# A row maximum that skips NaN: other piece sizes, fewer stores, and loads issued in turn from two queues

## The chip, the cores and the metric

The kernel runs on one core of a Trainium2 chip. Four of the core's engines matter here: ScalarE (ACT in the profile), GpSimd (POOL), VectorE (DVE) and SyncE (SP), which only issues DMA transfers. The data is moved by 16 DMA engines. The metric is the time of one execution on the device, in microseconds (us); the median of ten runs is given.

## The reference

```python
batch, seq, dim = 32, 2048, 2048
x = np.random.randn(batch, seq, dim).astype(np.float32)
mask = np.random.rand(batch, seq, dim) < 0.1
x[mask] = np.nan
...
return np.nanmax(x, axis=-1).astype(np.float32)
```

There are 65,536 rows of 2048 float32 numbers, 537 MB, of which a tenth are NaN. Of each row the largest number that is not NaN is returned (NaN for a row that has no other), so 65,536 results.

## The kernel before

**Groups and tiles.** A group is a block of consecutive rows of x, spread over the 128 partitions. A tile holds up to seven rows per partition, so 7 x 2048 numbers of 4 bytes in each partition, 7 MB in all; the buffers of this tile, `xt`, are three (pool `io`). There are 74 tiles in 13 groups. The table `TILES` says of each tile how it is loaded (rows per transfer), in which pieces it is converted (rows per piece), and in which groups of rows it is reduced. For example `([7], [1, 2, 2, -1, 1], [1, 2, 2, 2])` is one transfer of seven rows, five pieces, four reductions. The first tile has one row; 59 whole tiles of this kind follow, then a taper of 14 tiles with ever smaller transfers and pieces. Tiles are counted from 0 in this document.

**What is done to a piece.** [...] ScalarE reads the upper 16 bits of each number of a piece as an integer and writes a 16-bit key into a second buffer, `kt` (line 116; pool `mid`, four buffers of two rows). The key is an affine function of the upper half that has another slope for NaN patterns, so that turned back they are very low numbers. A second pass turns the key back and writes it over the upper half in `xt`: on GpSimd (line 133), or, for a piece with a minus sign in the table, on ScalarE (line 125). This second pass is called the write-back here. When all pieces under a group of rows are written back, VectorE takes their maximum (line 144) into the group's `acc`.

**End of a group.** VectorE marks rows that held nothing but NaN (line 155) and sets their bits to NaN (line 164) in `fin`; the store of `fin` is queued.

**Order.** Each engine works through its instructions in the order of its program and waits on semaphores for the others; a framework places the instructions and adds the waits. All loads are issued by SP (line 103), each as soon as VectorE has done the last reduction of the tile that had the same buffer three tiles earlier. SP also issues the stores (line 109, two groups late, between the loads; the last two at line 169).

Of the kernel before, what the change touches and what calls it, by code (L numbers as in the profile page):

```python
# [1 line left out]

# [4 lines left out]

TILES = (
    [([1], [1], [1])]
    + [([7], [1, 2, 2, -1, 1], [1, 2, 2, 2])] * 59
    + [([7], [2, 2, 1, 2], [4, 1, 2])]
    + [([7], [1, 2, 2, -2], [3, 2, 2])]
    + [([7], [1, 2, 2, 2], [3, 2, 2])]
    + [([7], [2, 2, 2, -1], [2, 2, 2, 1])]
    + [([2, 5], [1, 1, 2, 2, 1], [1, 1, 2, 2, 1])]
    + [([4, 3], [2, -2, 1, 1, 1], [2, 3, 2])]  # L20
    + [([4, 3], [2, 2, 2, -1], [2, 2, 3])] * 3
    + [([1, 3, 3], [1, 1, 1, 1, 2, -1], [1, 2, 1, 3])]
    + [([3, 2, 2], [1, 1, 1, 1, 1, 1, 1], [2, 1, 1, 1, 1, 1])]
    + [([2, 1, 2, 1, 1], [1, 1, -1, 1, 1, 1, 1], [3, 2, 1, 1])]
    + [([1, 1, 1, 1, 1, 1, 1], [1, 1, -1, 1, 1, 1, 1], [3, 1, 1, 1, 1])]
    + [([1, 1, 1, 1, 1, 1, 1], [1, 1, -1, 1, 1, 1, -1], [1, 2, 1, 1, 1, 1])]
)

GROUPS = [TILES[:7]] + [TILES[i : i + 6] for i in range(7, 73, 6)] + [TILES[73:]]
WIDE = 7  # L30
PIECE = 2

TOP = 0x7F7F
NAN = 0x7FC0
LOW = -129

EDGE = TOP + 0.25

NONE = -255.0 * 2.0**120


@with_exitstack
def kernel(
    ctx: ExitStack,
    tc: tile.TileContext,
    x: bass.AP,
    axis: bass.AP,
    out: bass.AP,  # L50
):

    nc = tc.nc
    P = nc.NUM_PARTITIONS
    f32, i32 = mybir.dt.float32, mybir.dt.int32
    i16, u16 = mybir.dt.int16, mybir.dt.uint16
    ALU = mybir.AluOpType
    ACT = mybir.ActivationFunctionType

    nd = len(x.shape)
    assert axis in (-1, nd - 1), axis
    D = x.shape[-1]  # L70

    xr = x.bitcast(i32).flatten_outer_dims()
    R = xr.shape[0]
    of = out.bitcast(i32).flatten_outer_dims().rearrange("r c -> (r c)")
    rows = [sum(sum(loads) for loads, _, _ in g) for g in GROUPS]
    assert R == P * sum(rows)

    io = ctx.enter_context(tc.tile_pool(name="io", bufs=3))
    mid = ctx.enter_context(tc.tile_pool(name="mid", bufs=4))
    res = ctx.enter_context(tc.tile_pool(name="res", bufs=3))  # L80
    sing = ctx.enter_context(tc.tile_pool(name="sing", bufs=1))
    flag = ctx.enter_context(
        tc.tile_pool(name="flag", bufs=2, space=bass.MemoryType.PSUM)
    )
    top = sing.tile([P, 1], f32)
    nc.vector.memset(top, EDGE)  # L86
    warm = sing.tile([P, 1], f32)
    nc.scalar.activation(out=warm, in_=top, func=ACT.Prelu, alpha=0.5)  # L88

    stores = []  # L90
    r0 = 0
    for s, g in zip(rows, GROUPS):
        xg = xr[r0 : r0 + P * s].rearrange("(p s) d -> p (s d)", p=P)
        og = of[r0 : r0 + P * s].rearrange("(p s) -> p s", p=P)
        r0 += P * s
        acc = res.tile([P, s], f32, tag="acc")
        base = 0
        for loads, pieces, reds in g:
            assert sum(loads) == sum(abs(c) for c in pieces) == sum(reds)
            xt = io.tile([P, WIDE * D], i32, tag="xt")  # L100
            at = 0
            for c in loads:
                nc.sync.dma_start(  # L103
                    out=xt[:, at * D : (at + c) * D],
                    in_=xg[:, (base + at) * D : (base + at + c) * D],
                )
                at += c
            if len(stores) > 1:
                nc.sync.dma_start(**stores.pop(0))
            at = done = 0  # L110
            reds = list(reds)
            for c in pieces:
                back, c = c < 0, abs(c)
                xp = xt[:, at * D : (at + c) * D]
                kt = mid.tile([P, PIECE * D], u16, tag="kt")
                nc.scalar.activation(  # L116
                    out=kt[:, : c * D],
                    in_=xp.bitcast(i16)[:, 1::2],
                    func=ACT.Prelu,
                    bias=top,  # L120
                    scale=-1.0,
                    alpha=float(TOP - LOW) / (EDGE - NAN),
                )
                if back:
                    nc.scalar.activation(  # L125
                        out=xp.bitcast(i16)[:, 1::2],
                        in_=kt[:, : c * D],
                        func=ACT.Copy,
                        bias=float(TOP),
                        scale=-1.0,  # L130
                    )
                else:
                    nc.gpsimd.tensor_scalar(  # L133
                        out=xp.bitcast(i16)[:, 1::2],
                        in0=kt[:, : c * D],
                        scalar1=-1.0,
                        scalar2=float(TOP),
                        op0=ALU.mult,
                        op1=ALU.add,
                    )  # L140
                at += c
                while reds and done + reds[0] <= at:
                    n = reds.pop(0)
                    nc.vector.tensor_reduce(  # L144
                        out=acc[:, base + done : base + done + n],
                        in_=xt[:, done * D : (done + n) * D]
                        .bitcast(f32)
                        .rearrange("p (c d) -> p c d", c=n),
                        axis=mybir.AxisListType.X,
                        op=ALU.max,  # L150
                    )
                    done += n
            base += at
        none = flag.tile([P, s], i32, tag="none")
        nc.vector.tensor_scalar(  # L155
            out=none,
            in0=acc,
            scalar1=NONE,
            scalar2=float(0x00C00000),
            op0=ALU.is_equal,  # L160
            op1=ALU.mult,
        )
        fin = res.tile([P, s], i32, tag="fin")
        nc.vector.tensor_tensor(  # L164
            out=fin, in0=acc.bitcast(i32), in1=none, op=ALU.bitwise_or
        )
        stores.append(dict(out=og, in_=fin))
    for st in stores:
        nc.sync.dma_start(**st)


# [1 line left out]
_INS = ['x', 'axis']  # L173
_OUTS = [((32, 2048), 'float32')]

_NUMBERS = {'axis': -1}


# [26 lines left out]
```

## Time and profile before

| | us |
|---|---|
| median of 10 runs | 1262.38 (1262.19 to 1262.47) |
| the profiled execution, its own time | 1262.31 |
| its span in the profile | 1260.5 |
| VectorE busy | 1127.1 |
| ScalarE busy | 1123.5 |
| GpSimd busy | 1063.0 |
| ScalarE idle before line 116, waiting for a load | 126.0 |

The span runs from the first to the last instruction of the program on the core; the time of an execution has a little around it (here 1.8 us). Busy times of the engines overlap, so they don't add up to the span. The DMA engines moved 537.25 MB, 426 GB/s over the span. In the views, a row of a group ends with the number of instructions, their busy time in us and the mean of one in ns, and the idle time of the engine before them with what ended it.

### The profile page before, as it was taken

Reading aid. Unit: us, or ns where it says so; the run is one execution under the profiler, and the core shown is the slowest. Engines: PE = TensorE matmul, PEld = TensorE weight load, DVE = VectorE, ACT = ScalarE, POOL = GpSimd, SP = SyncE. Lnnn points to the kernel's source line nnn. Section 1 sums busy time; section 2 is a strip of 40 time slices with the busy share of each in tenths; the row PEclk is TensorE's granted clock in tenths of the full one; section 3 lists DMA queues with packets and bytes.
Section 4 is the critical chain, followed back from the end, with each engine's and each line's share of the span. In section 5 each row is a group of like instructions: output and inputs, shape, how many; then the busy total and the mean of one; then the engine's idle time right before and its main releaser. Section 6 shows DMA issues by size and latency. Waiting matters only on the chain.

```text
span 1260.5 us, 1707 instructions
## 1 busy us (share of the span) xinstructions
DVE 1127.1 (89%) x319; ACT 1123.5 (89%) x440; POOL 1063.0 (84%) x302
## 2 busy tenths in 40 slices
DVE  1888998989899998889999898898989879999999
ACT  3898998889899888889889888998888989899997
POOL 2888888888888888888888888888888888998996
DMA  9999999999999999999999999999999999999995
GB/s 412 437 437 437 433 426 422 437 437 437 434 435 435 425 428 437 434 437 435 435 434 426 426 437 435 437 436 433 433 419 437 435 437 435 418 434 430 426 421 211
DMA packets 16141, 537.25 MB, mean 426 GB/s; under 512 B 3456, under 2 KB 3456, under 8 KB 3456
## 3 DMA queue, kind: packets, MB, share of 16 engines
q1 hardware_dynamic: 16128, 537.14, 98.9%
q14 instruction: 13, 0.11, 0.0%
HBM read 536.87 MB, written 0.26 MB: 426 GB/s over the span
## 4 chain that ended last, share of the span: by engine, by line
DMA 51%; POOL 15%; ACT 14%; DVE 10%; issue 9%; SPq 0%; DVEq 0%; ACTq 0%
DMA xt<-in_x_dram 51%; POOL xt L133 15%; ACT kt L116 13%; DVE acc L144 10%; ACT xt L125 1%; SPq L103 0%; DVEq L144 0%; DVE none L155 0%; ACTq L116 0%; DVE fin L164 0%; ACTq L125 0%
## 5 line engine op out<-in xcount | busy, mean ns | idle before, releaser
L144 DVE TENSOR_REDUCE acc<-xt 128x2 f32<-128x4096 f32 (+2 forms) x292 | 1122.8, 3889 | 129.5 <-POOL xt L133 129.3
L133 POOL TENSOR_SCALAR xt<-kt 128x2048 int16<-128x2048 uint16 (+1 forms) x298 | 1062.8, 3567 | 189.3 <-ACT kt L116 175.9
L116 ACT ACTIVATE kt<-xt,top 128x2048 uint16<-128x2048 int16 (+1 forms) x368 | 951.2, 2658 | 128.5 <-DMA xt<-in_x_dram 126.0
L125 ACT ACTIVATE xt<-kt 128x2048 int16<-128x2048 uint16 x70 | 177.7, 2539 | 0.3
L155 DVE TENSOR_SCALAR none<-acc 128x42 int32<-128x42 f32 (+2 forms) x13 | 2.6, 202 | 0.5
L164 DVE TENSOR_TENSOR fin<-acc,none 128x42 int32<-128x42 int32 (+2 forms) x13 | 2.6, 196 | 0.4
L88 ACT ACT_TABLE_LOAD x1 | 1.3, 1283 | 0.7 <-PEq L186 0.7
L86 DVE MEMSET top<- 128x1 f32 x1 | 0.1, 59 | 0.8 <-PEq L186 0.8
L186 POOL MEMSET const-float32-0.0<- 128x1 f32 x1 | 0.1, 98 | 0.2 <-issue 0.2
L88 ACT ACTIVATE warm<-top 128x1 f32<-128x1 f32 x1 | 0.2, 202 | 0.0
L186 POOL MEMSET const-bfloat16-1.0<- 128x1 bf16 x1 | 0.1, 101 | 0.0
L186 POOL MEMSET const-uint8-127<- 128x1 uint8 x1 | 0.1, 101 | 0.0
L186 POOL MEMSET const-float32-1.0<- 128x1 f32 x1 | 0.1, 98 | 0.0
## 6 DMA issues: line engine op xcount, KB each, us to landing
xt<-in_x_dram SPq DMA_DIRECT2D x63, 7168.0 KB, 26.7
xt<-in_x_dram SPq DMA_DIRECT2D x7, 3072.0 KB, 25.6
xt<-in_x_dram SPq DMA_DIRECT2D x19, 1024.0 KB, 20.8
xt<-in_x_dram SPq DMA_DIRECT2D x4, 4096.0 KB, 19.6
xt<-in_x_dram SPq DMA_DIRECT2D x5, 2048.0 KB, 27.6
xt<-in_x_dram SPq DMA_DIRECT2D x1, 5120.0 KB, 23.2
out_dram<-fin SPq DMA_DIRECT2D x11, 21.0 KB, 26.5
out_dram<-fin SPq DMA_DIRECT2D x1, 21.5 KB, 26.8
```

The lines of the kernel that those rows point to most:

```text
L86: nc.vector.memset(top, EDGE)
L88: nc.scalar.activation(out=warm, in_=top, func=ACT.Prelu, alpha=0.5)
L116: nc.scalar.activation(out=kt[:, : c * D], in_=xp.bitcast(i16)[:, 1::2], func=ACT.Prelu, bias=top, scale=-1.0, alpha=float(TOP - LOW) / (E ...
L125: nc.scalar.activation(out=xp.bitcast(i16)[:, 1::2], in_=kt[:, : c * D], func=ACT.Copy, bias=float(TOP), scale=-1.0,)
L133: nc.gpsimd.tensor_scalar(out=xp.bitcast(i16)[:, 1::2], in0=kt[:, : c * D], scalar1=-1.0, scalar2=float(TOP), op0=ALU.mult, op1=ALU.add,)
L144: nc.vector.tensor_reduce(out=acc[:, base + done : base + done + n], in_=xt[:, done * D : (done + n) * D] .bitcast(f32) .rearrange("p (c d ...
L155: nc.vector.tensor_scalar(out=none, in0=acc, scalar1=NONE, scalar2=float(0x00C00000), op0=ALU.is_equal, op1=ALU.mult,)
L164: nc.vector.tensor_tensor(out=fin, in0=acc.bitcast(i32), in1=none, op=ALU.bitwise_or)
L186: nc = _bacc.Bacc("TRN2", target_bir_lowering=False, num_devices=1)
```

## The change

The table of tiles is another one: the 57 whole tiles up to the taper are converted in pieces of two, three and two rows (three instructions on ScalarE in place of five), and the reductions match the pieces. In every third of them ScalarE writes back the last piece, two rows; in the others GpSimd writes back all seven. Before, ScalarE wrote back one row of every such tile. The key buffers hold three rows and are three in number; a piece is put into the buffer in use if it still fits. There are six groups instead of 13, each with an `acc` of its own, on which the marking works in place, and all stores stand after the loop in the program text. Loads are written into the program two tiles ahead of the tile that is worked on, and whole-tile loads are issued in turn by SP and by ScalarE; a tile that is loaded in several transfers stays with the queue whose turn it is and leaves the turn there.

```diff
+    + [
+        ([7], [2, 3, 2], [2, 3, 2]),
+        ([7], [2, 3, 2], [2, 3, 2]),
+        ([7], [2, 3, -2], [2, 3, 2]),
+    ] * 19
+    + [([7], [2, 3, 2], [2, 3, 2])] * 2
+    + [([1, 6], [-1, 3, 1, -2], [4, 3])]
+    + [([7], [3, 2, -2], [3, 4])]
+    + [([7], [2, 2, 3], [2, 2, 3])] * 2
+    + [([7], [2, 1, 2, 2], [2, 1, 2, 2])]
+    + [([5, 2], [1, 1, 1, 2, -1, 1], [1, 1, 1, 3, 1])]
...
-GROUPS = [TILES[:7]] + [TILES[i : i + 6] for i in range(7, 73, 6)] + [TILES[73:]]
+GROUPS = [TILES[:14]] + [TILES[i : i + 12] for i in range(14, 74, 12)]
 WIDE = 7
-PIECE = 2
+
+KEYS = 3
...
-    mid = ctx.enter_context(tc.tile_pool(name="mid", bufs=4))
-    res = ctx.enter_context(tc.tile_pool(name="res", bufs=3))
+    mid = ctx.enter_context(tc.tile_pool(name="mid", bufs=3))
+    res = ctx.enter_context(tc.tile_pool(name="res", bufs=1))
...
+    ready = []
+    queues = [nc.sync, nc.scalar]
+
+    def fetch():
+
+        xg, base, loads = ahead.pop(0)
+        xt = io.tile([P, WIDE * D], i32, tag="xt")
+        queue = queues[0]
+        if len(loads) == 1:
+            queues.reverse()
+        at = 0
+        for c in loads:
+            queue.dma_start(
+                out=xt[:, at * D : (at + c) * D],
+                in_=xg[:, (base + at) * D : (base + at + c) * D],
+            )
+            at += c
+        ready.append(xt)
+
+    stores = []
+    used = KEYS
...
-            xt = io.tile([P, WIDE * D], i32, tag="xt")
-            at = 0
-            for c in loads:
-                nc.sync.dma_start(
-                    out=xt[:, at * D : (at + c) * D],
-                    in_=xg[:, (base + at) * D : (base + at + c) * D],
-                )
-                at += c
-            if len(stores) > 1:
-                nc.sync.dma_start(**stores.pop(0))
+            while len(ready) < 3 and ahead:
+                fetch()
+            xt = ready.pop(0)
...
-                kt = mid.tile([P, PIECE * D], u16, tag="kt")
+                if used + c > KEYS:
+                    kt = mid.tile([P, KEYS * D], u16, tag="kt")
+                    used = 0
+                kp = kt[:, used * D : (used + c) * D]
+                used += c
                 nc.scalar.activation(
-                    out=kt[:, : c * D],
+                    out=kp,
...
-        fin = res.tile([P, s], i32, tag="fin")
-        nc.vector.tensor_tensor(
-            out=fin, in0=acc.bitcast(i32), in1=none, op=ALU.bitwise_or
-        )
-        stores.append(dict(out=og, in_=fin))
+        bits = acc.bitcast(i32)
+        nc.vector.tensor_tensor(out=bits, in0=bits, in1=none, op=ALU.bitwise_or)
+        stores.append(dict(out=og, in_=bits))
     for st in stores:
         nc.sync.dma_start(**st)
```

The rest of the taper's table is changed in the same manner and left out here.

## The prediction

> **What bounds the kernel now.** I read the page first: engine shares, then the slices.
>
> ```profile
> DVE 1127.1 (89%) x319; ACT 1123.5 (89%) x440; POOL 1063.0 (84%) x302
> DMA  9999999999999999999999999999999999999995
> GB/s 412 437 437 437 433 426 422 437 437 437 434 435 435 425 428 437 434 437 435 435 434 426 426 437 435 437 436 433 433 419 437 435 437 435 418 434 430 426 421 211
> q1 hardware_dynamic: 16128, 537.14, 98.9%
> ```
>
> No engine is full, but the DMA engines are busy in every slice but the last, on one queue, at up to 437 GB/s. The transfer sets the time. In the timeline ScalarE starts successive tiles at 481.19, 498.12 and 515.07, so a seven-row load takes T = 16.94 us. Then the chain of waits, one loop of a buffer (start, length, what):
>
> ```profile
> 498.06 0.02 ACTq L116
> ...
> 498.12 5.61 ACT kt L116 x2
> ...
> 503.81 4.76 POOL xt L133
> ...
> 508.65 4.78 POOL xt L133
> ...
> 517.78 4.42 DVE acc L144
> ...
> 522.22 27.32 DMA xt<-in_x_dram
> ...
> 549.62 5.61 ACT kt L116 x2
> ```
>
> A tile that landed at 498.1 is reduced at 522.2, a hold of 24.1, and at once the next load into its buffer is issued. That load lands 27.3 later though it needs 16.94: it stands behind the load in front. This standing time is what keeps the DMA full. Its limit: three buffers make 3T = 50.8; a load that finds the engines idle needs T + 1.9 (the packet records have the first bytes 1.0 after the first issue, and a landing seen 0.85 after a typical engine's last byte). So a hold may last 50.8 - 18.8 = 32.0. Now 8 us are spare. Who holds the loads back is in the waits of the DMA queue (us in total, times, longest):
>
> ```profile
> SPq L103 <- DVE acc L144: 950.5, 59, 24.1
> ```
>
> Prices, from the groups by form (mean ns after the comma):
>
> ```profile
> L144 DVE TENSOR_REDUCE acc<-xt 128x2 f32<-128x4096 f32 x199 | 873.3, 4416 | 95.8 <-POOL xt L133 95.8
> L133 POOL TENSOR_SCALAR xt<-kt 128x4096 int16<-128x4096 uint16 x142 | 676.8, 4766 | 79.5 <-ACT kt L116 73.3
> L116 ACT ACTIVATE kt<-xt,top 128x4096 uint16<-128x4096 int16 x144 | 525.2, 3694 | 8.5 <-DMA xt<-in_x_dram 8.5
> L116 ACT ACTIVATE kt<-xt,top 128x2048 uint16<-128x2048 int16 x224 | 438.3, 1992 | 120.1 <-DMA xt<-in_x_dram 117.6 <-POOL xt L133 2.5
> L133 POOL TENSOR_SCALAR xt<-kt 128x2048 int16<-128x2048 uint16 x156 | 386.1, 2475 | 109.8 <-ACT kt L116 102.6
> L144 DVE TENSOR_REDUCE acc<-xt 128x3 f32<-128x6144 f32 x9 | 58.9, 6548 | 3.3 <-POOL xt L133 3.2
> L125 ACT ACTIVATE xt<-kt 128x4096 int16<-128x4096 uint16 x2 | 9.5, 4770 | 0.1
> ```
>
> Last, how ScalarE's queue treats a wait; the write-back's line, between 519 and 536:
>
> ```profile
> L125 ACTq EVENT_SEMAPHORE  x1: 17/17/17, 519.7 to 519.7; - x1
> L125 ACT ACTIVATE xt<-kt x1: 2470/2470/2470, 528.0 to 528.0; 128x2048 int16<-128x2048 uint16 x1
> ```
>
> The queue was past the write-back's first wait 8.3 us before it ran, so it runs ahead of the datapath; but the ACTq record of 498.06 shows that it stands still at a tile's first activation until that tile has landed. I assume that a load in this queue does likewise: it can overtake activations still executing, not a wait in front of it.
>
> **What the Trainium skill says.** "DMA: Bandwidth & Descriptors", Queues, rings and completion order: SP and ACT own one ring each on the same 16 DMA engines, and an engine with work on both takes packets from them in turn. The run before has one data queue and can't show it. Same page, Where 436 GB/s comes from: a ceiling of 435 GB/s; the best slices have 437, so a second queue finds no spare rate. "Perfetto Trace Analysis", DMA Instruction — HWDGE (DVE, Sync): the issuing sequencer waits for the semaphores itself; the 950.5 us of SP agree.
>
> **The change part by part.**
>
> *Stores*: 12 inside the stream become 5 (the built order puts those five between SP's loads, only the last behind them), plus one at the end in both. A store lengthens a loop of the chain by 0.1 to 0.7 (26.64 without, 27.32 with): 7 x 0.4 = -3 us. A store now has twice the bytes and as many rows; bounds -5 to 0.
>
> *Pieces.* A three-row activation isn't in the trace: at least the two-row 3.69, at most 3 x 1.99 = 5.98; the step from one to two rows is 1.70, so 5.40. On GpSimd the step is 2.29: 7.06 (4.77 to 7.43). A 2,3,2 tile with all its write-back on GpSimd costs it 4.77 + 7.06 + 4.77 = 16.6, as much as T; every third tile costs it 11.8. Over six tiles GpSimd has 90.0 + 1.3 of handovers, VectorE 92.3, ScalarE 86.3, all under 6T = 101.6, so none becomes the bound by sum. But the hold grows: 3.7 (ScalarE, two rows) + 16.6 + 4.4 (VectorE) + 0.3 = 25.0 if GpSimd is free at landing, near 30 where it isn't. These edits cost nothing while the hold stays under 32.0.
>
> *Write-back.* In the built order of ScalarE the write-back of 18 of the 19 tiles that have one stands behind the next tile's first activation, which waits for that tile's landing. Such a tile holds its buffer for T + 3.7 + 4.8 + 4.4 = 29.9 at the least. Every other time (tiles 9, 15, 21...) VectorE also reduces the next tile's first piece before it, and a load stands in ScalarE's queue between.
>
> *Loads on ScalarE.* Tiles 1, 3, 5 ... 59, 62 and 64 are loaded from there. Nine of these (11, 17 ... 59) stand behind the first activation of the tile before: issued when the load in front has already landed, they restart an idle DMA, 1.9 us each. Issue itself (0.33 on SP) is hidden beside activations.
>
> *Two rings.* A load issued while another runs takes half the rate from it. Work is conserved, but the load in front lands later by as much as it had left, and holds everything behind its landing.
>
> I follow engines and queues in the built order, each instruction starting when its engine is free and its last input there. The same count of the order before gives 1261.3 against a span of 1260.5. After the start the new order repeats every six tiles; from tile 16's landing as 0:
>
> - Load 17 (ScalarE) issued at 0, lands 18.8.
> - ScalarE: 16's first piece to 3.7, 15's write-back to 8.4, 16's others to 13.7 and 17.3. VectorE, still busy with 15's middle to 10.5, reduces 16's first to 14.8, 15's last to 19.1: tile 15 held for 38. Load 18 (SP) issued there, 2.1 us of idle DMA after load 17's last byte.
> - GpSimd ends 16 at 25.7, VectorE at 31.8: load 19 issued (ScalarE). Load 18 has 4.2 left, which takes 8.5 shared: lands 42.3.
> - GpSimd runs 17 from 25.7 to 42.5, VectorE ends it at 48.6: load 20 (SP). Load 19 has 4.4 left: lands 59.3.
> - 18's write-back waits for that: 59.3 + 3.7 + 4.7, reduced at 72.2: load 21 (ScalarE), 2.3 idle after load 20, which lands 71.8. Load 21 lands 91.1.
> - 19's second piece waits behind that write-back (to 73.0), GpSimd to 85.0, VectorE to 91.1: load 22 (SP), 1.9 idle; lands 109.9.
>
> So 109.9 in place of 101.6: 8.3 lost per six tiles, eight times from tile 10 to tile 58: +66. The start: loads 1 and 2 share the engines, so tile 1 lands at 36.5 (before, 22.6), is done at 63.6, and the DMA idles 9.7 from 55.0 for want of a buffer; tile 10 is 10.6 late. After tile 58: one more restart (1.9), and 6.3 idle before load 64, which waits for tile 61: +8. The end behind the last landing (12.1 before), with VectorE more behind: +3. Stores -3. Sum 66 + 11 + 8 + 3 - 3 = +85: a span of 1345.5. The profiled execution took 1262.31 with a span of 1260.5, and the median of runs is 1262.38, so I add 1.9: **1347 us**, 6.7% slower.
>
> **Rivals.**
> 1. *Loads keep their order*: the load in front keeps the engines. For: SP alone does so now. Against: the skill's page. The cycle then is 105.6 (restart of load 17 and late load 18 alone), the start costs nothing: +32, 1295.
> 2. *ScalarE's queue waits for the activations in front of a load to end.* For: no run shows a load there. Against: the 8.3 us of running ahead. Each blocked load comes 3.7 later, others too: the count gives +20 more, 1367.
> 3. *Not slower*: two rings together carry more than one. In the same count, break-even is at T = 14.4, 510 GB/s; nothing above 437 is in the slices. If it did, 1255 or so.
> 4. Three-row prices at their bounds: GpSimd at 7.43 and ScalarE at 5.98 give 1358, at 5.5 and 4.5 they give 1334 (1280 with rival 1).
>
> **How the numbers follow.** Shared rings as counted 0.64 (1325 to 1362); rival 1, or something between it and sharing, 0.22 (1278 to 1325); rival 2 0.09; a milder loss, 1265 to 1278, 0.02; rival 3 0.03. The range 1284 to 1368 leaves out about 0.15. A measurement tells about 0.2% (2.5 us) from no change; faster 0.02, same 0.01, slower 0.97.
>
> **What would show it.** Two data queues; slices near 400 GB/s instead of 435, the second one far lower; ScalarE's loads landing 19 to 27 us after issue; ScalarE waiting for landings much longer than 126 us; write-backs of two rows starting right behind a landing; three-row GpSimd at 7.06. Wrong, if a seven-row load in the middle lands at intervals of 16.94 throughout (holds below 32), or if loads of both queues in flight land one T apart (no sharing).

## The result and the profile after

The changed kernel takes 1350.99 us (median; 1347.58 to 1353.88), before 1262.37 on the same chip: a ratio of 1.0705, 95% interval 1.0695 to 1.0714. The prediction was 1347, 6.7% slower. Its profiled execution has a span of 1351.7 us.

The page of the changed kernel, engine shares, slices and data queues:

```profile
DVE 1116.7 (83%) x242; ACT 1053.5 (78%) x281; POOL 1090.0 (81%) x219
DMA  9999999999989989999998999998999999799995
GB/s 411 434 406 434 382 382 431 382 382 407 389 378 414 431 363 386 433 380 384 407 395 366 431 404 387 382 433 367 393 417 399 380 408 434 330 432 434 426 427 235
q1 hardware_dynamic: 10080, 302.26, 52.8%
q10 hardware_dynamic: 4608, 234.88, 41.2%
```

VectorE and ScalarE do less work than before, GpSimd 27 us more (1063.0 before), and none of the three is busy for more than 83% of the span. The rate falls to 363 to 395 GB/s in more than half of the slices between start and taper, and returns to 426 to 434 in the taper, but for one slice with 330. So most of the loss is in the stretch of whole tiles, and it is lost transfer time. The second queue is q10. The shares of the queues say more: the 16 engines were busy for 94.0% of 1351.7 us, before for 98.9% of 1260.5. So they stood still for 81 us in place of 14, and the same bytes took them 1271 us in place of 1247. Of the 91 us of loss in the profile, 67 are idle DMA engines and 24 are packets that took longer.

The waits of the DMA queue of SP, and those of ScalarE, in the changed kernel (us in total, times, longest):

```profile
SPq L117 <- DVE acc L175: 973.6, 36, 37.9
ACT kt L147 <- DMA xt<-in_x_dram: 273.3, 56, 20.6
```

ScalarE waits 273 us for landings in place of 126. The 37.9 can't be set beside the 24.1 of before, as SP now has only every second load: the run below with write-backs in their place and two queues has the same 37.9 and loses nothing in the middle. The holds can be compared. From the landing of a tile to the issue of the next load into its buffer, the median is 31.8 us and the longest 39.5; before, both were 24.2. The prices of the new forms (count, busy us, mean ns):

```profile
L164 POOL TENSOR_SCALAR xt<-kt 128x6144 int16<-128x6144 uint16 x63 | 443.3, 7037 | 115.1 <-ACT kt L147 110.9 <-DVE acc L175 1.8
L147 ACT ACTIVATE kt<-xt,top 128x6144 uint16<-128x6144 int16 x63 | 340.3, 5402 | 19.8 <-POOL xt L164 12.6 <-DMA xt<-in_x_dram 7.2
L156 ACT ACTIVATE xt<-kt 128x4096 int16<-128x4096 uint16 x21 | 99.7, 4750 | 2.2 <-DVE acc L175 2.1
```

7.04, 5.40 and 4.75: those of the prediction were 7.06, 5.40 and 4.77. Its six-tile cycle can be read in the chain of waits. Tile 16 lands at 293.3, tile 22 at 404.4:

```profile
293.36 19.42 DMA xt<-in_x_dram
...
312.86 12.18 ACT kt L147 x3
325.04 27.72 DMA xt<-in_x_dram
...
352.84 3.71 ACT kt L147
356.55 4.65 ACT xt L156
361.20 5.27 ACT kt L147
...
384.52 19.85 DMA xt<-in_x_dram
...
404.48 19.61 DMA xt<-in_x_dram
```

Three of the transfers shown take 19.4 to 19.9 from issue to landing: they were issued when the load in front had landed, or half a microsecond before it. Before, the seven-row loads of tiles 4 to 59 took 26.3 to 27.6, some 10 us of that standing in line. The middle lines are the late write-back: tile 19 lands at 352.8, its first piece runs, then 18's write-back, and only then its own second piece. The landings of the cycle, counted from tile 16's:

| load of tile | 17 | 18 | 19 | 20 | 21 | 22 |
|---|---|---|---|---|---|---|
| predicted | 18.8 | 42.3 | 59.3 | 71.8 | 91.1 | 109.9 |
| measured | 19.5 | 42.6 | 59.5 | 72.6 | 91.8 | 111.1 |

How ScalarE's queue handles a load shows in the timeline (start, us, engine, line):

```profile
293.34 3.71 ACT L147 ACTIVATE kt<-xt,top 128x4096 uint16<-128x4096 int16 x1 [5.17 <-DMA xt<-in_x_dram]
293.36 0.33 ACTq L117 DMA_DIRECT2D xt<-in_x_dram  x1
...
296.95 4.75 ACT L156 ACTIVATE xt<-kt 128x4096 int16<-128x4096 uint16 x1
```

The load of tile 17 is issued 0.02 us after the activation in front of it has begun, not after it has ended, but it could not be issued before tile 16 had landed. VectorE had freed its buffer 3.3 us earlier. Nine loads are held back in this way (11, 17 ... 59), by 2.7 to 3.3 us each. This decides rival 2.

That the two rings share the engines can be read from loads 18 and 19, the only two issued between 309 and 330:

```profile
L117 SPq DMA_DIRECT2D xt<-in_x_dram x1: 328/328/328, 311.2 to 311.2; - x1
L117 ACTq DMA_DIRECT2D xt<-in_x_dram x1: 334/334/334, 325.0 to 325.0; - x1
...
DMA to landing us min/median/max: 24.6/26.1/27.7
```

Load 18 was issued 1.5 us before load 17 landed, and landed 24.6 later, at 335.8. Load 17, which had the engines to itself, took 19.4; five loads of the run below with all write-backs late and no load blocked, issued 1.6 to 2.0 us before the landing in front and undisturbed after it, took 19.3 to 19.8. So load 18 lost some 5 us to the load issued 13.8 after it, which a queue in order would not have allowed. The taking of turns that the Trainium skill describes ("DMA: Bandwidth & Descriptors", Queues, rings and completion order) is there. The packets of the first loads, in the last section, show the turns themselves.

### The profile page after: what moved, and what is told of

It is laid out like the page before. It is cut to its first block, busy times and chain, and to the rows that moved or that the text cites. A ratio compares the mean times of both kernels' runs of the same rounds, so it can differ in the third digit from the quotient of the medians.

```text
span 1351.7 us, 1217 instructions
## 1 busy us (share of the span) xinstructions
DVE 1116.7 (83%) x242; ACT 1053.5 (78%) x281; POOL 1090.0 (81%) x219
## 4 chain that ended last, share of the span: by engine, by line
DMA 53%; ACT 21%; DVE 11%; POOL 9%; issue 5%; SPq 0%; ACTq 0%; DVEq 0%
DMA xt<-in_x_dram 53%; ACT kt L147 17%; DVE acc L175 11%; POOL xt L164 9%; ACT xt L156 4%; SPq L117 0%; ACTq L147 0%; DVE acc L195 0%; DVE none L186 0%; ACTq L117 0%; DVEq L175 0%
## 5 line engine op out<-in xcount | busy, mean ns | idle before, releaser
L164 POOL TENSOR_SCALAR xt<-kt 128x4096 int16<-128x4096 uint16 (+2 forms) x215 | 1089.8, 5069 | 252.1 <-ACT kt L147 238.9
L147 ACT ACTIVATE kt<-xt,top 128x4096 uint16<-128x4096 int16 (+2 forms) x247 | 930.3, 3822 | 286.4 <-DMA xt<-in_x_dram 273.3
L156 ACT ACTIVATE xt<-kt 128x4096 int16<-128x4096 uint16 (+1 forms) x32 | 127.1, 3972 | 2.5 <-DVE acc L175 2.1
## 6 DMA issues: line engine op xcount, KB each, us to landing
xt<-in_x_dram SPq DMA_DIRECT2D x31, 7168.0 KB, 23.2
xt<-in_x_dram SPq DMA_DIRECT2D x13, 1024.0 KB, 22.5
xt<-in_x_dram SPq DMA_DIRECT2D x1, 6144.0 KB, 19.9
```

The source lines that it names most:

```text
L147: nc.scalar.activation(out=kp, in_=xp.bitcast(i16)[:, 1::2], func=ACT.Prelu, bias=top, scale=-1.0, alpha=float(TOP - LOW) / (EDGE - NAN),)
L156: nc.scalar.activation(out=xp.bitcast(i16)[:, 1::2], in_=kp, func=ACT.Copy, bias=float(TOP), scale=-1.0,)
L164: nc.gpsimd.tensor_scalar(out=xp.bitcast(i16)[:, 1::2], in0=kp, scalar1=-1.0, scalar2=float(TOP), op0=ALU.mult, op1=ALU.add,)
```

## The experiments

The theory had three parts that come together in the changed program: late write-backs, ScalarE's loads that wait for a landing ("blocked"), and two rings. The prediction gave most of the loss to the rings: without sharing (its rival 1) it counted 32 of 85 us. The experiments take the parts one by one. In the edits shown, the arguments are shortened: `NO_SYNC` is an order that the framework keeps without adding a semaphore.

**All loads on SP.**

```diff
-    queues = [nc.sync, nc.scalar]
+    queues = [nc.sync, nc.sync]
```

> All loads from SP; pieces, table, groups and buffers as changed. In the order that the framework now builds, each write-back of ScalarE stands right behind its piece, and all six stores stand behind the last load. Theory (two rings together with late write-backs and blocked loads push holds past 32): the hold of every tile is 27.4 by the count, so the DMA never idles in the middle: 1258 us (1255 to 1262), a little under before, landings 16.94 apart. Rival (the pieces of two and three rows alone are too long for three buffers, whatever the queue): 1295 or more, DMA idle in the middle.

1261.36 us, ratio to before 0.9992 (0.9983 to 1.0001): the whole loss is gone, and the gain of 4 us that was counted isn't there; 1 us or nothing. The median hold is 27.3. The pieces, buffers and groups of the change cost nothing by themselves. The framework that places the instructions reacts to the loads on ScalarE: without them it puts each write-back right behind its piece. So this one word undoes two things, and the next runs separate them.

**The old pieces with two queues.** The changed program with the table of before.

> The changed program with its two queues, key buffers and six groups, but the old table of pieces (1, 2, 2, 1, 1, one row written back by ScalarE in each whole tile). Theory: holds are 24.1 as before, so two rings alone cost nothing after the start: 1260 with the start as the changed kernel really has it, 1270 if loads 1 and 2 share from the beginning. Rival (two rings alone cost 4% or more, by lower rate or by restarts): 1310 or more.

1264.39 us, 1.0017 (1.0011 to 1.0024), between the two figures of the theory. Two rings alone cost 2 us. The median hold is 24.1 here and no load is blocked. Loads do share: between tiles 10 and 58 landings follow each other at 12.7 to 21.2 us, but at 17.0 in the mean, as before the change. So neither the new pieces nor the second queue loses much alone.

**Write-backs in their place, two queues.** An order without a semaphore is added on ScalarE:

```diff
+                if last is not None:
+                    tc.add_manual_dep(key.ins, last, NO_SYNC, reason="order")
+                    last = None
                 if back:
-                    nc.scalar.activation(
+                    wb = nc.scalar.activation(
...
+                    last = wb.ins.name
```

> The changed kernel, two queues, with one added order on ScalarE: a write-back stands before the next key activation of the program. The loads then stand behind the last piece of a tile and not behind the next tile's landing, too. Theory: holds 27.4, no idle in the middle: 1261 (1258 to 1273), nearly all of the loss gone. Rival (sharing of the engines by two rings is enough for the loss, whatever the order on ScalarE): 1320 or more.

1269.28 us, 1.0055 (1.0040 to 1.0070), in the stated range. 82 of the 89 us are gone with both queues still in use. Sharing is not enough for the loss. The 7 us left are not in the middle: tile 10 lands at 179.8 here and at 174.9 with one queue, tile 58 at 995.5 and 989.8. Some 5 are lost at the start, the rest behind.

**Late write-backs, one queue.** All loads on SP, and each two-row write-back ordered behind the next tile's first key activation:

```diff
+                if late is not None and late[1] is not xt:
+                    tc.add_manual_dep(late[0], key.ins.name, NO_SYNC, reason="order")
+                    late = None
...
+                    if loads == [7] and pieces == [2, 3, -2]:
+                        late = (wb.ins, xt)
```

> All loads from SP, and every write-back of the 19 tiles of 2, 3 and 2 rows is put behind the first key activation of the next tile, as in the changed kernel. Theory: the hold is 31.7 by the count, just under the limit of 32.0 of the prediction; 1258 if that limit is right; the changed kernel's restarts took about 0.6 longer than counted, which would put the limit at 31.4 and cost up to 0.3 to 0.6 for each of 57 tiles: 1275 to 1295. Rival (a late write-back alone brings the whole loss): 1340 or more.

1302.25 us, 1.0313 (1.0288 to 1.0337), above both ranges of the theory and below the rival. The late write-backs alone cost 41, with one ring. This was the surprise: by the prediction's limit (32.0) they should have been free. A loop of this run, in its chain of waits:

```profile
318.83 21.20 DMA xt<-in_x_dram
...
343.73 4.75 ACT xt L167
348.48 5.27 ACT kt L148
...
353.82 7.05 POOL xt L177
...
360.89 4.89 DVE acc L188
...
367.36 4.42 DVE acc L188
...
371.80 21.71 DMA xt<-in_x_dram
```

The tile lands at 340.0 and is free at 371.8: a hold of 31.8, as counted (the median of the run is 31.7). But the loads take 21.2 and 21.7, not 18.8, although these two are issued 3 us before the load in front has landed (the median of the run is 4.1). 31.8 + 21.7 = 53.5 is three times 17.8, and 17.77 is the mean interval of landings here, 16.94 the full rate.

An idle DMA is the smaller part of this loss. The queue's bytes and share of time, with the write-backs in place (span 1259.4) and late (span 1303.4), one ring in both:

```profile
q1 hardware_dynamic: 14688, 537.14, 98.9%
```

```profile
q1 hardware_dynamic: 14688, 537.14, 97.7%
```

The engines stand still for 30 us in place of 14, and are busy for 1273 us in place of 1246 with the same packets. So 16 of the 44 us between these two executions are idle time, and 28 are packets that took longer.

**Late write-backs of one row, one queue.** As the run before, with another table:

```diff
-        ([7], [2, 3, -2], [2, 3, 2]),
+        ([7], [2, 3, 1, -1], [2, 3, 2]),
```

> As the run with late write-backs on one queue (1302), but ScalarE writes back one row in place of two in every third tile (its last piece is cut into two of one row, GpSimd writes back the other), so the late write-back takes 2.5 in place of 4.75. The hold by the count is 29.4, between the 27.3 of the run on one queue that lost nothing and the 31.7 of the run that lost 0.83 us per load. If a load must be issued 21.5 us before its landing, as that run's loads took, the limit is 50.8 - 21.5 = 29.3, and this run is on it: 1261 to 1268. If the limit is the 32.0 of the prediction and the 41 us came from something else in the late order: 1290 or more, as there. If loads begin to lose gradually from 27.4 on: 1275 to 1285.

1261.06 us, 0.9990 (0.9983 to 0.9997). The write-back is as late as in the run before, but 2.3 us shorter, and 41 us are gone. The median hold is 29.35 (27.3 with write-backs in place, 31.7 with two rows late). The seven-row loads of these runs on one queue, write-backs in place, late with one row, late with two rows (the last number is the median from issue to landing):

```profile
xt<-in_x_dram SPq DMA_DIRECT2D x63, 7168.0 KB, 23.5
```

```profile
xt<-in_x_dram SPq DMA_DIRECT2D x63, 7168.0 KB, 21.6
```

```profile
xt<-in_x_dram SPq DMA_DIRECT2D x63, 7168.0 KB, 21.7
```

From a hold of 27.3 to 29.4, the load gives up 1.9 us of standing in line, and nothing is lost. From there to 31.7 it has nothing left to give: some 21.6 is what a load takes. The limit of the hold lies between 29.4 and 31.7 by these runs, and 50.8 - 21.6 = 29.2 puts it near the lower end. Of the versions run this has the lowest median, 0.1% below before.

**Loads first, two queues.** On ScalarE the load of tile n+1 is ordered before the first key activation of tile n, so that none is blocked.

```diff
+                if at == 0 and ahead_load is not None:
+                    tc.add_manual_dep(key.ins, ahead_load, NO_SYNC, reason="order")
```

> The changed kernel, two queues, with one added order on ScalarE: the load of tile n+1, where it is ScalarE's, stands before the first key activation of tile n, so none waits for a landing. In the order that is built then, two of every three write-backs still stand behind the next tile's first activation, one in its place. Theory (late write-backs and two rings): by the count 1292, and with loads on the edge dearer than counted, as in the run with late write-backs on one queue, 1292 to 1325. Rival (the blocked loads are the cause): 1265 or less. Rival (they are no part of it): 1345 or more.

1311.19 us, 1.0384 (1.0368 to 1.0400), in the range of the theory. 40 us back, but nine of the 19 write-backs (tiles 9, 15 ... 57) went into their place too, more than expected. So the same with all of them late:

> Two queues; all write-backs of the tiles of 2, 3 and 2 rows behind the next tile's first key activation, as changed; but ScalarE's load of tile n+1 stands before the first key activation of tile n, so that no load waits for a landing. Beside the run with late write-backs on one queue (1302) and the changed kernel (1351) it splits their difference. Theory of the prediction (sharing by two rings makes it, the blocked loads are only where it shows): 1335 to 1350. Rival (the blocked loads make it): 1302 plus the 5 to 8 us that two rings cost with early write-backs, 1305 to 1315.

1317.62 us, 1.0447 (1.0426 to 1.0467): 33 us less than the changed kernel, with all write-backs late and both rings in use. The rival is the nearer one: 33 of the 49 us between one queue with late write-backs (1302) and the changed kernel (1351) are the blocked loads; the second ring has 15. Both are differences of a few runs that spread over 6 to 8 us. The queues' shares say what a blocked load does: in this run the engines stand still for 3.3% of 1313.0, 43 us, in the changed kernel for 81, and they are busy for 1270 us in both. So the blocked loads cost idle DMA time. Of the 9.6 us between this profiled execution and that of the late run on one queue, 0.8 are there by tile 10, and 6.3 come behind tile 58, where loads 62 and 64 are still ScalarE's.

**Blocked loads, write-backs in their place, two queues.** The order of the run of 1269, and in addition the loads of tiles 11, 17 ... 59 each behind the first key activation of the tile before. These are the nine that are blocked in the changed kernel.

```diff
+            if n < 9 or n > 59 or n % 6 != 4:
+                behind = None
...
+                if at == 0 and behind is not None:
+                    tc.add_manual_dep(behind, key.ins.name, NO_SYNC, reason="order")
```

> Two queues and write-backs in their place (the run of 1269), but two of three of ScalarE's loads stand behind the first key activation of the tile before and so wait for its landing, with some 15 to 18 such loads over the run. Each restarts an idle DMA: 1.9 to 2.6 us for each, 1269 plus 30 to 45, 1299 to 1314, whatever the rings do. Rival (a blocked load is caught up by the next, which then stands longer in line): 1270 to 1280.

1311.93 us, 1.0393 (1.0377 to 1.0408): +43 for blocked loads with the write-backs in place, at the upper end of what was expected. But they are more, and blocked longer, than in the changed kernel. After VectorE had freed their buffers, the nine chosen loads waited 4.6 to 5.4 us, and eight others (13, 19 ... 55), which this built order puts behind a landing too, 6.8 to 8.2: 103 us in all, of which 43 were lost. In the changed kernel it was 27 us on nine loads. Together:

| write-backs | loads | rings | us |
|---|---|---|---|
| in place | free | one | 1261.4 |
| in place | free | two | 1269.3 |
| late | free | one | 1302.3 |
| in place | blocked, 17 loads | two | 1311.9 |
| late | free | two | 1317.6 |
| late | blocked, 9 loads | two (the change) | 1351.0 |

Late write-backs cost 41 with one ring and 48 with two, blocked loads 33 with late write-backs, two rings 8 to 15. The 43 of blocked loads with write-backs in place is not the same quantity as the 33, so that the sums come near each other proves little. A load can be blocked only in ScalarE's queue: none was blocked with one ring, so the 33 includes whatever sharing a blocked load sets off. All loads on ScalarE would show blocked loads on one ring; that was not run.

**First four loads from SP, two queues, write-backs in place.**

```diff
+        first = len(ahead) > len(TILES) - 5
-        if len(loads) == 1:
+        if len(loads) == 1 and not first:
```

> The changed kernel with the write-backs in their place, as in the earlier run that gave 1269, and the first four loads all from SP, the turns beginning with the fifth. Theory (the rest of that run's loss is at the start, where two rings share while the buffers are first filled): 1262 to 1265. Rival (it is spread over the run): 1269.

1271.41 us, 1.0069 (1.0056 to 1.0083): no gain. Tiles 0 to 3 land as before the change, but tile 4 lands at 77.4 in place of 73.4 and tile 10 at 182.3. From tile 10 to tile 58 landings are 16.97 apart, and nothing more is lost. So the loss isn't spread over the run, nor is it bound to the first four loads; it comes soon after the turns begin. Why was not followed further.

**Six groups alone.** The kernel before, with only the groups, the marking in place and the stores after the loop. Of the edit, the groups:

```diff
-GROUPS = [TILES[:7]] + [TILES[i : i + 6] for i in range(7, 73, 6)] + [TILES[73:]]
+GROUPS = [TILES[:14]] + [TILES[i : i + 12] for i in range(14, 74, 12)]
```

> The kernel before with only the six groups, the marking in place in an acc of its own for each group, and all stores after the loop; the old pieces, four key buffers, loads from SP. In the built order all six stores stand behind the last load. Theory: 12 stores taken out of the stream at 0.1 to 0.6 each, 1257 to 1261. Rival (stores were hidden anyway): 1262, no difference.

1261.77 us, 0.9995 (0.9987 to 1.0003): no difference that can be told. The last load lands at 1248.0, before at 1248.4. The stores in the stream had cost next to nothing.

## Why the prediction was right or wrong

*The sign and the size* were right: 1347 against 1351. The mechanism in the large was right too: holds grow past what three buffers allow, and the DMA, which sets the time, runs dry. The order of events was right: in the cycle of six tiles all six landings came within 1.2 us of the count, and it took 111.1 against 109.9. But the DMA ran dry for only 67 of the 91 us of loss in the profile; packets that took longer, which the count didn't have, made the rest. That the sum came within 4 us is in part luck, as its errors had both signs (below).

*Prices of the new forms*: right to 0.02 us. Rival 4 falls.

*ScalarE's queue*: right. A load overtakes activations that are executing and stands behind a wait. Rival 2 falls.

*The limit of the hold* was mis-sized. The step is the price of a load without standing room: T + 1.9 = 18.8, put together from the first bytes and a landing in the packet records. In the changed kernel, loads issued half a microsecond before the landing in front or later, and undisturbed after it, took 19.3 to 19.9. On one ring, with late write-backs, loads issued 2.1 to 4.3 us before the landing in front took 20.0 to 22.3, mostly 21.6. That is T + 4.7, and makes the limit of the hold some 29.2 in place of 32.0. What the 4.7 consists of is not shown.

*The split between causes* failed, as a consequence. With a limit of 32.0 late write-backs alone (31.7) were just free, so in the count it took blocked loads and, above all, the sharing of the rings to lose time: rival 1, the same order without sharing, was put at 1295, 52 below. Measured, late write-backs cost 41 with one ring, and the second ring 8 to 15. In that run six tiles took 106.6 us, where the limit of 32.0 gives 101.6. Rival 1 itself, with its blocked loads, was not run without the second ring. The nine blocked loads were priced at 1.9 each; taking the blocking away with late write-backs gave 33. Each had waited 2.7 to 3.3, 27 in all.

*The start*: predicted 10.6 late at tile 10, measured 180.8 - 175.2 = 5.6. The idle 9.7 us at 55 didn't come, and the second slice, forecast low, has 434. Loads 1 and 2 did not share at once, as loads 0 and 1 did: see the last section. *The stretch from tile 10 to tile 58* took 889 in place of 816: 73 more, against 66 less the stores' share. *From tile 58 to the last landing* it lost 11, against 8. *The end* behind the last landing took 13.5, 1.4 more than before and not 3. *The stores*: -3 predicted; the run with six groups shows 0.6 or nothing.

*Rival 3* falls. Single slices of runs with two rings have up to 448 GB/s, but so has one of a run with one ring (446). With two rings and nothing else in the way (the old pieces), landings were 17.0 apart in the mean, as before.

## What to carry to other kernels

Where loads wait for buffers, look at how long before the landing in front a load can be issued. With one ring this kernel lost nothing at a median of 4.5 us, and 0.8 us per load at a median of 4.1. Loads put on ScalarE changed the order of its other instructions here, and stood behind its waits; read the built order, not the program text. A piece that is written back behind the next tile's first activation holds its buffer until that tile has landed; here that made the hold 4.4 us longer. A DMA queue that loses time need not be idle; compare its busy time for the same bytes as well.

## What was not expected of the hardware

Two rings take turns by packets, not by bytes. The first load has one row, 1 MB in pieces of 8 KB; beside it runs ScalarE's first load, 7 MB in pieces of 56 KB. Before, the small load landed 4.9 us after its issue. In the changed kernel's timeline, from the start of the span:

```profile
0.74 0.41 ACTq L117 DMA_DIRECT2D xt<-in_x_dram  x1
0.74 0.85 SPq L117 DMA_DIRECT2D xt<-in_x_dram  x2
...
23.26 10.91 ACT L147 ACTIVATE kt<-xt,top 128x2048 uint16<-128x2048 int16 x3 [20.59 <-DMA xt<-in_x_dram]
```

It lands at 23.2, 22.5 after its issue, together with the load seven times its size: in the packet records, groups of sixteen pieces of 8 KB and sixteen of 56 KB alternate, eight of each, which reads as each of the 16 engines taking one piece from either ring in turn (the records don't name the engine). Both loads have 128 pieces, and so the small one took the time of the large one.

How the loss grows shows in the run with late write-backs on one ring, tiles 5 to 58. The 19 loads issued 4.3 us or more before the landing in front landed 17.06 us after it on average, the 17 issued 3.6 to 4.3 before it 17.64 after, and the 18 issued 2.1 to 3.6 before it 18.63 after. It is odd that a load behind another on the same ring is the slower one: four of the five issued 2.1 to 2.6 us before the landing in front took 21.3 to 21.6 us, while on the other ring those issued 1.6 to 2.0 before it took 19.3 to 19.8, as said above.

In the packet records of that run, 1130 of the 8064 packets of 56 KB took over 2.2 us, 2.4 in the median of these and up to 3.9, in place of 2.12; with write-backs in place there are seven. The 16 engines end load 18 of that run 2 us apart; in the run with one row late, which lost nothing, they end loads 10 and 19 within 0.5 and 1.1 us. That this spread makes the loss was not tested.
